# When a layer's state-space tables are built, and where its delta rule starts: one reordering inside a hybrid decoder layer

## The chip, the cores and the metric

The program runs on one core of a Trainium2 chip. The metric is the device time of one execution in microseconds. A core has five engines that take instructions in order, each from its own list: TensorE (PE, with its weight loads shown apart as PEld), VectorE (DVE), ScalarE (ACT), GpSimd (POOL) and SyncE (SP), which here issues the DMAs. They meet through semaphores: an instruction that waits holds up everything behind it on its own engine.

## The reference, cut to what matters

Two layers run over 512 positions of width 1024. In each layer a mixer splits one projection of the normalized input into four head groups, each 256 wide; an expert layer (PEER) with a large pair of tables follows, then a gated embedding. The PEER part fills most of the time and is not touched. The mixer is:

```
y_ret  = retention(rq, rk, rv, rg, ...)                 # group A
y_lru  = rglru(lg, lx, ...)                             # group B
y_s5   = s5(su, a_re, a_im, b.., c.., d, log_dt, glu..) # group C
y_gdn  = gated_deltanet(dqkv, db, da, dg, ...)          # group D
mixed = concatenate([rmsnorm(y, branch_norm[l, j]) for j, y in enumerate(groups)])
h = h + mixed @ w_out[l]
```

Group C (S5) is a diagonal complex recurrence. Its coefficients do not depend on the data, only on the layer's parameters: powers of exp(a dt), the input matrix B and the output matrix C multiplied by them. From these the kernel builds tables. Group D (the gated DeltaNet) needs the convolved q, k, v and two gate logits per head (db, da); it inverts a triangular matrix per chunk of 64 positions and then carries a state from chunk to chunk.

## The kernel before

All float32 products are made of three products of split halves (hi*hi, lo*hi, hi*lo), so a weight that is used has first been loaded into `wraw` and split by ACT (`whi`) and DVE (`wlo`). The work is written as Python generators: each `yield` ends a step, and `mix` takes steps from several generators in proportion to a weight (a weight of 2 has twice as many steps per round as one of 1). What `mix` and `take` write down is still reordered: the program is scheduled once, when it is built, so each engine's list is fixed before the run, and what an engine does at run time follows that list.

`mixer` (from L1723) makes one layer's mixer in two halves.

First half: `proj` multiplies z with 11 column blocks of `w_in`, 8 steps per block (`pj`, PSUM tiles `ps_j`). Each block hands its result to a consumer: blocks 1 to 3 to the convolution of q, k, v of D (`d_cons_qkv`), the fourth (column 2560) to the gates of D (`d_cons_g`), the next four to A, then B and, last, C. Beside it runs the first part of D (`gen_D` up to `d_prepared`, PSUM tiles `ps_d`) and of A.

Second half: C (`gen_C`, then `finish_T`), the rest of A, B, an embedding product (`gen_embed`) and the rest of D (tiles dX, dE, dAT, oD, PSUM `ps_d`). Then `residual` multiplies the four finished groups (`zm`) with `w_out` (PSUM `ps_r`) and adds to `h`; its banks are those of `ps_j`, so it begins when the work on those is done. Its first six row blocks (`early=6`) are those of A, B and C, which need nothing of D. The query projection of PEER (`ps_q`) follows.

The tables of C are made by `gen_Cprep` (the argument `prep`, L1094): some 165 DVE instructions with a few of the other engines, on tiles s5raw, sb, s5p, sp, sq. It saves them to a DRAM buffer `Td`; `c_load` (L1077, L1082) loads them back as `s5t`. Layer 0 has its `prep` inside the mixer's first half; layer 1's tables are made elsewhere, and its mixer has no `prep`. `take(pj, 2 + 24)` stands ahead of it: that is 26 of the projection's 90 steps, three blocks and the start.

gen_C uses the tables thus: products of the inputs by `s5t` (L356) with copies and transposes (L1269, L1273, L1276), complex rotations and two scans per half (DVE L341, L344, L347, L1287, tiles sx, sZ, zm), output products, transposes (L1308), a gate product (`gluw`), and a norm whose result `xb` is turned (L1047) into `zm`.

Of the kernel before, what the change touches and what calls it, by code (L numbers as in the profile page):

```python
# [25 lines left out]
D = 1024  # L26
# [165 lines left out]
def drain(*gens):  # L192

    live = [[g, w] for g, w in gens]
    while live:
        for e in list(live):
            for _ in range(e[1]):
                try:
                    next(e[0])
                except StopIteration:  # L200
                    live.remove(e)
                    break
# [39 lines left out]
class Ker:  # L242
# [201 lines left out]
    def proj(self, z, wap, blocks, pool, bank, wmax=256, lo_eng=None, per=2, early=0):  # L444
# [15 lines left out]
        def spl(x):  # L460
            if x // 2 >= NB:
                return
            n = blocks[x // 2][1]
            hi = pool.tile([P, 4, wmax], F32R, name="whi", tag="whi", bufs=3)
            lo = pool.tile([P, 4, wmax], F32R, name="wlo", tag="wlo", bufs=3)
            self.split(hi[:, :, :n], lo[:, :, :n], raws.pop(x)[:, :, :n], lo_eng if x % 2 == 0 else None)
            sp[x] = (hi, lo)
            load(x + self.WR)
# [41 lines left out]
        for i, (c0, n, kind, cons) in enumerate(blocks):  # L510
            if begun and i < 2:
                continue
            nj = n // P if kind == "C" else NTB
            for j in range(nj):
                ps = bank()
                for kd in range(KD):
# [3 lines left out]
                    f, e = kd == 0, kd == KD - 1  # L520
                    if kind == "C":
                        cs = slice(j * P, (j + 1) * P)
# [6 lines left out]
                    if e:  # L529
                        cons(j, ps)  # L530
                        if j == 0:
                            spl(2 * i + 2)
                    if (kd + 1) % (per if kind == "C" else 2 * per) == 0:
                        yield
# [858 lines left out]
    def gen_select(self, pool, rpool, bank_s, qT, subT, tb, res):  # L1393
# [58 lines left out]
        def tree(x, out, eng):  # L1452
            n = 16
            while n > 2:
                n //= 2
                eng.tensor_tensor(x[:, 0:n], x[:, 0 : 2 * n : 2], x[:, 1 : 2 * n : 2], op=ALU.add)
            eng.tensor_tensor(out, x[:, 0], x[:, 1], op=ALU.add)

        M = t2("tM", [16, P], BF16)
        W = t2("tW", [16, P], BF16)  # L1460
        W2 = t2("tW2", [16, P], BF16)
# [4 lines left out]
        yield  # L1466
        self.mul(v4(W), v4(M), perh(dl))
        tree(W, fl(sel[:, 0]), V)
        yield
        self.sub(fl(bv), fl(pf), st)  # L1470
        self.tt(M, over(bv), self.t_row, ALU.is_equal)
        self.mul(v4(W), v4(M), perh(sb[:, 1]))
        tree(W, fl(sel[:, 1]), V)
        yield
# [50 lines left out]
    def peer(self, l, z, sides, prep=None):  # L1525
# [3 lines left out]
        with ExitStack() as c0:  # L1529
# [6 lines left out]
            def cons(b0):  # L1536
                def f(j, ps):
                    self.mul(qT[:, b0 + j, :], ps, z.rb)
                return f

            pj = self.proj(z, self.ap["wq"][l], [(256 * i, 256, "C", cons(2 * i)) for i in range(4)], wp, lambda: qbank())
            self.take(pj, 2)
# [175 lines left out]

    PD, PC, BD = 0, 0, 4
    R2, RC2, LO = 0.7, 0.4, 0  # L1720
    R0, R1, RC, RA = 2, 2, 0.6, 0.4

    def mixer(self, l, z, Td, gain, opened, sides, Pd, prep=None):  # L1723
        sa, sb = sides
        self.l, self.z, self.a_ready, self.c_half, self.d_half = l, z, False, False, False
        win = self.ap["w_in"][l]
        with ExitStack() as c0:
            cm_ = c0.enter_context(ExitStack())
            mx = self.pool(cm_, "mx", sb)
            self.a_alloc(mx)  # L1730
            self.b_alloc(mx)
            self.c_alloc(mx)
            oC = self.xb.rearrange("p a b -> p (a b)").rearrange("p (t c) -> p t c", t=NTB)
            cd_, cj_ = c0.enter_context(ExitStack()), c0.enter_context(ExitStack())
            bd = banks(self.pool(cd_, "ppd", space=PSUM, side="right"), "d", self.BD)
            bj = banks(self.pool(cj_, "ppj", space=PSUM, side="left"), "j", 8 - self.BD)
            cD = cm_.enter_context(ExitStack())
            with ExitStack() as c1:
                dcp = self.pool(c1, "dcp", sa)
                self.d_alloc(mx, dcp)  # L1740
                wp = self.pool(c1, "wp", sa)
                self.cvpool = wp
                blocks = [(1792, 256, "C", self.d_cons_qkv(0)), (2048, 256, "C", self.d_cons_qkv(2)), (2304, 256, "C", self.d_cons_qkv(4)),
                          (2560, 264, "T", self.d_cons_g), (0, 256, "T", self.a_cons("q")), (256, 256, "T", self.a_cons("k")),
                          (512, 256, "T", self.a_cons("v")), (768, 256, "T", self.a_cons("g")),
                          (1280, 256, "C", self.b_cons_x), (1024, 256, "C", self.b_cons_g), (1536, 256, "C", self.c_cons)]
                pj = self.proj(z, win, blocks, wp, bj, wmax=264, lo_eng=self.G if prep is not None and self.LO else None)
                if prep is not None:
                    with ExitStack() as c2:
                        np_ = self.pool(c2, "np", sa)  # L1750
                        self.take(pj, 1)
                        first = lambda part: self.z_first(z, self.gain("mixg", l), bd, np_, part)
                        first(0)
                        self.load_mix(mx, l)
                        first(1)
                else:
                    self.load_mix(mx, l)
                self.take(pj, 2 + 24)
                with ExitStack() as c2:
                    self.rope_tables(mx, self.pool(c2, "pr", sb))  # L1760
                if prep is not None:
                    with ExitStack() as c2:
                        self.mix([(prep(self.pool(c2, "pk", sb), bd), 1), (pj, self.R0)])
                self.take(pj, 8)
                dp = self.pool(cD, "dp", sb)
                self.d_prepared = False
                D = self.gen_D(dp, dcp, bd)

                def d1():
                    while not self.d_prepared:  # L1770
                        self.take(D, 1)
                        yield

                def a1():
                    while not self.a_ready:
                        yield
                    yield from self.gen_A(mx, dcp, bj, self.aq)

                D1 = d1()
                self.mix([(pj, 1), (a1(), self.R2), (D1, self.R1, self.PD)])  # L1780
                drain((D1, 1))
            z.ctx.close()
            self.zm = Mixed(self.pool(c0, "zm", sa))
            self.oD = self.pool(c0, "od", sa).tile([P, NTB, 256], F32, name="oD")
            with ExitStack() as c1:
                cp = self.pool(c1, "cp", sa)
                self.c_load(cp, Td)
                oA, yB = self.aq, self.lg

                def c_():  # L1790
                    yield from self.gen_C(l, cp, bj, oC)
                    yield from self.finish_T(cp, bj, oC, 4, "C")

                def a_():
                    yield from self.norm_A(cp, oA)
                    yield from self.finish_T(cp, bj, oA, 0, "A")

                def b_():
                    yield from self.gen_B(l, cp, bj, yB)
                    yield from self.finish_B(cp, bj, yB)  # L1800

                def upto(g, flag):
                    while not getattr(self, flag):
                        self.take(g, 1)
                        yield

                C = c_()
                W = self.gen_embed(l, self.pool(c1, "em", sa), bj, Pd)
                self.mix([(upto(C, "c_half"), self.RC), (a_(), self.RA), (b_(), self.RA), (W, self.RA), (upto(D, "d_half"), 1)])
                drain((upto(D, "d_half"), 1))  # L1810
                self.mix([(C, self.RC2), (D, 1, self.PD)])
            wp = self.pool(c0, "rw", sa)
            pj = self.residual(self.zm, self.ap["w_out"][l], wp)
            self.take(pj, 2)
            cj_.close()
            with ExitStack() as c1:
                self.rbank = banks(self.pool(c1, "rp", space=PSUM, side="left"), "r", 8 - self.BD)
                self.take(pj, 8)
                drain((D, 1))
                cm_.close()  # L1820
                cd_.close()
                znew = opened()
                self.blockwise(pj, znew, gain, banks(self.pool(c1, "rt", space=PSUM, side="right"), "t", 2), wp, 0)
# [202 lines left out]
```

## Time and profile before

| | us |
|---|---|
| median of 3 runs | 3987.49 (3984.82 to 3992.34) |
| the profiled execution | 3988.84 |
| its span in the profile | 3987.0 |
| first projection of layer 0 to its q projection | 10.2 to 396.8 |
| first projection of layer 1 to its q projection | 1998.5 to 2360.1 |

The span is what the profile's time axis covers; 1.8 us of the time lie outside it. Rows below give start and length in us within it, and the tiles by the names of the program (output<-input). A row of one line and form may stand for several instructions in a row (x4). A bracket at the end tells how long the engine was idle before the row and what ended that.

### The profile page before, as it was taken

Reading aid. Unit: us, or ns where it says so; the run is one execution under the profiler, and the core shown is the slowest. Engines: PE = TensorE matmul, PEld = TensorE weight load, DVE = VectorE, ACT = ScalarE, POOL = GpSimd, SP = SyncE. Lnnn points to the kernel's source line nnn. Section 1 sums busy time; section 2 is a strip of 40 time slices with the busy share of each in tenths; the row PEclk is TensorE's granted clock in tenths of the full one; section 3 lists DMA queues with packets and bytes.
Section 4 is the critical chain, followed back from the end, with each engine's and each line's share of the span. In section 5 each row is a group of like instructions: output and inputs, shape, how many; then the busy total and the mean of one; then the engine's idle time right before and its main releaser. Section 6 shows DMA issues by size and latency. Waiting matters only on the chain.

```text
span 3987.0 us, 54319 instructions
## 1 busy us (share of the span) xinstructions
PE 3891.8 (98%) x20648; PEld 3231.3 (81%) x20648; DVE 2899.9 (73%) x5889; ACT 1533.8 (38%) x2245; POOL 552.0 (14%) x470
## 2 busy tenths in 40 slices
PE   7999999999999999999999999999999999999998
PEld 6878888878888888888898787777788888888887
DVE  9785899968888666555575769998588865555555
ACT  4454255652233232222443443566422222222223
POOL 4321000010001222222031210000100012222220
PEclk9999999999999999999999999999999999999999
DMA  4223255675653443333231133556756534333422
GB/s 146 71 78 106 77 198 177 241 269 184 202 170 121 145 129 130 122 111 121 82 102 59 58 122 103 191 209 232 247 184 201 166 102 136 110 121 108 134 83 90
DMA packets 317190, 562.33 MB, mean 141 GB/s; under 512 B 18176, under 2 KB 206720, under 8 KB 311552
## 3 DMA queue, kind: packets, MB, share of 16 engines
q1 hardware_dynamic: 316928, 558.86, 42.0%
q8 instruction: 162, 2.65, 0.3%
q14 instruction: 100, 0.82, 0.1%
HBM read 443.96 MB, written 114.83 MB: 140 GB/s over the span
## 4 chain that ended last, share of the span: by engine, by line
PE 87%; DVE 9%; DMA 2%; issue 1%; ACT 1%; POOL 0%; SPq 0%; DVEq 0%; POOLq 0%; ACTq 0%
PE ps_v L356 35%; PE ps_u L356 32%; PE ps_j L356 5%; PE ps_g L356 5%; PE ps_d L356 3%; PE ps_r L356 2%; PE ps_q L356 2%; DVE ulo L360 1%; DVE to L338 1%; PE ps_s L356 1%; DMA s5t<-Td 1%; DVE wlo L360 0%; DVE dc L350 0%; DMA wraw<-in_ple_wg_dram 0%; PE ps_t L373 0%
## 5 line engine op out<-in xcount | busy, mean ns | idle before, releaser
L1685 DVE TENSOR_TENSOR h<-h,ps_v 128x512 f32<-128x512 f32 x1024 | 678.0, 682 | 633.1 <-PE ps_v L356 631.9
L356 PE MATMUL ps_v<-vhi,whi 128*128 128x512 f32 x2048 | 800.6, 391 | 18.8 <-ACT whi L359 18.8
L356 PE MATMUL ps_u<-zhi,ulo 128*128 128x512 f32 x2048 | 812.9, 397 | 0.6 <-DVE ulo L360 0.6
L356 PE MATMUL ps_u<-zhi,uhi 128*128 128x512 f32 x2048 | 809.9, 395 | 0.4 <-ACT aout L353 0.4
L356 PE MATMUL ps_u<-zlo,uhi 128*128 128x512 f32 x2048 | 808.2, 395 | 0.0
L356 PE MATMUL ps_v<-vlo,whi 128*128 128x512 f32 x2048 | 800.3, 391 | 0.0
L356 PE MATMUL ps_v<-vhi,wlo 128*128 128x512 f32 x2048 | 796.4, 389 | 0.0
L360 POOL TENSOR_TENSOR ulo<-uraw,uhi 128x1024 fp32r<-128x1024 f32 x136 | 329.4, 2423 | 2191.1 <-ACT uhi L359 1614.3
L359 ACT CAST uhi<-uraw 128x1024 fp32r<-128x1024 f32 x256 | 269.7, 1054 | 854.5 <-PE ps_u L356 571.2
L359 ACT CAST whi<-dact 128x512 fp32r<-128x512 f32 x256 | 158.5, 620 | 818.4 <-issue 376.1
L356 PEld LDWEIGHTS ps_v<-vhi,whi 128*128 128x128 f32 x2048 | 385.5, 188 | 102.0 <-ACT whi L359 19.6
L356 PEld LDWEIGHTS ps_u<-zhi,ulo 128*128 128x128 f32 x2048 | 384.8, 188 | 84.2 <-DVE ulo L360 1.4
L356 PEld LDWEIGHTS ps_u<-zlo,uhi 128*128 128x128 f32 x2048 | 384.9, 188 | 83.5
L356 PEld LDWEIGHTS ps_u<-zhi,uhi 128*128 128x128 f32 x2048 | 384.9, 188 | 83.0 <-ACT aout L353 1.2
L356 PEld LDWEIGHTS ps_v<-vlo,whi 128*128 128x128 f32 x2048 | 385.9, 188 | 81.6
L356 PEld LDWEIGHTS ps_v<-vhi,wlo 128*128 128x128 f32 x2048 | 384.9, 188 | 81.2
L341 DVE TENSOR_TENSOR dact<-dact,dg 128x512 f32<-128x512 f32 x256 | 320.0, 1254 | 29.5 <-ACT dact L353 17.0
L360 DVE TENSOR_TENSOR vlo<-vraw,vhi 128x1024 fp32r<-128x1024 f32 x256 | 309.1, 1226 | 26.1 <-ACT vhi L359 26.1
L353 ACT ACTIVATE tstg<-ps_g 128x512 f32<-128x512 f32 x256 | 264.2, 1156 | 128.2 <-PE ps_g L356 126.1
L359 ACT CAST vhi<-vraw 128x1024 fp32r<-128x1024 f32 x256 | 261.6, 1048 | 21.8 <-PE ps_v L356 20.4
L360 DVE TENSOR_TENSOR wlo<-dact,whi 128x512 fp32r<-128x512 f32 x256 | 180.2, 706 | 37.1 <-ACT whi L359 24.1
L338 DVE TENSOR_TENSOR to<-t_iota,tii 128x1024 f16<-128x1024 bf16 x256 | 172.8, 685 | 2.0 <-ACT tii L353 1.7
(470 smaller groups left out, 5382.4 us busy)
## 6 DMA issues: line engine op xcount, KB each, us to landing
uraw<-in_uT_dram SPq DMA_DIRECT2D x256, 512.0 KB, 3.4
vraw<-in_v_dram SPq DMA_DIRECT2D x256, 512.0 KB, 3.9
Gd<-tstg SPq DMA_DIRECT2D x32, 2048.0 KB, 7.2
dg<-Gd SPq DMA_DIRECT2D x64, 1024.0 KB, 6.0
Ad<-aout SPq DMA_DIRECT2D x120, 256.0 KB, 2.2
dact<-Ad SPq DMA_DIRECT2D x120, 256.0 KB, 3.4
wraw<-in_w_in_dram SPq DMA_DIRECT2D x40, 512.0 KB, 3.6
wraw<-in_w_out_dram SPq DMA_DIRECT2D x16, 512.0 KB, 3.8
```

Of the source, the lines that this page charges most:

```text
L338: (eng or self.V).tensor_tensor(out, a, b, op=op)
L341: (eng or self.V).tensor_tensor(out, a, b, op=ALU.mult)
L353: self.A.activation(out, x, f, **k)
L356: self.PE.matmul(out, l, r, start=start, stop=stop)
L359: self.A.copy(hi, x)
L360: (lo_eng or self.V).tensor_tensor(lo, x, hi.bitcast(F32), op=ALU.subtract)
L1685: self.reached = V.tensor_tensor(self.h[:, tb, ds], self.h[:, tb, ds], ps, op=ALU.add).ins
```

## The change

In layer 0 the call that mixes `prep` with the projection goes away; so `take(pj, 8)` follows `take(pj, 2 + 24)` directly and D begins after 34 steps, right behind the block of its gates, where before at least 34 more steps lay between. `prep` now runs in the second half in a mix with A, B, the embedding and the first part of D's rest (`d_half`), with a weight of 0.6 in place of 2. Behind it stand, in a pool of their own, the loading of the tables and C. In layer 1, where `prep` is None, the same lines give nearly the same order as before.

```diff
-    R0, R1, RC, RA = 2, 2, 0.6, 0.4
+    R0, R1, RC, RA = 0.6, 2, 0.6, 0.4
...
-                if prep is not None:
-                    with ExitStack() as c2:
-                        self.mix([(prep(self.pool(c2, "pk", sb), bd), 1), (pj, self.R0)])
                 self.take(pj, 8)
...
-                self.c_load(cp, Td)
...
-                C = c_()
-                W = self.gen_embed(l, self.pool(c1, "em", sa), bj, Pd)
-                self.mix([(upto(C, "c_half"), self.RC), (a_(), self.RA), (b_(), self.RA), (W, self.RA), (upto(D, "d_half"), 1)])
-                drain((upto(D, "d_half"), 1))
+                Dh = (upto(D, "d_half"), 1)
+                gs = [(a_(), self.RA), (b_(), self.RA), (self.gen_embed(l, self.pool(c1, "em", sa), bj, Pd), self.RA)]
+                if prep is not None:
+                    with ExitStack() as c2:
+                        self.mix([(prep(self.pool(c2, "pk", sa), bj), self.R0)] + gs + [Dh])
+                    gs = []
+                cc = self.pool(c1, "cc", sa)
+                self.c_load(cc, Td)
+                C = c_(cc)
+                self.mix([(upto(C, "c_half"), self.RC)] + gs + [Dh])
+                drain(Dh)
                 self.mix([(C, self.RC2), (D, 1, self.PD)])
```

PE, DVE, POOL and SP issue the same instructions in both kernels; only the order differs.

TensorE's list in layer 0 before, in the stretch where the gate product of C and its turned result stand. Between the matmuls of C (`ps_j<-gluw`, `ps_j<-ca,xb`) lie those of D (`ps_d`), and those of the residual (`ps_r`) begin among D's.

```order
L356 MATMUL ps_j<-gluw,sx_2357 128x512 x5
L718 MATMUL ps_d<-ca,dX 128x128 x2
L356 MATMUL ps_d<-dX,dE 128x128 x2
...
L1047 MATMUL ps_j<-ca,xb 128x128 x4
L718 MATMUL ps_d<-ca,dX 128x128 x2
L1047 MATMUL ps_j<-ca,xb 128x128 x4
L356 MATMUL ps_d<-dX,dE 128x128 x2
L356 MATMUL ps_d<-dS,dwT 64x128
L356 MATMUL ps_d<-dAT,dX 128x128 x8
L356 MATMUL ps_d<-dS,dwT 64x128
L356 MATMUL ps_r<-whi,zm_2567 128x256 x4
L718 MATMUL ps_d<-ca,dX 128x128 x2
```

The same list in the change, from D's last rows to the residual's first. The lines left out repeat the first pair of C three times and its middle once.

```order
L356 MATMUL ps_d<-dvn,daT 64x64 x2
L820 MATMUL ps_d<-ca,oD 128x128 x4
L356 MATMUL ps_j<-s5t_2872,sx_2900 128x256 x2
L1273 MATMUL ps_j<-ca,sx_2899 128x128 x4
...
L356 MATMUL ps_j<-s5t_2875,su 128x128
L356 MATMUL ps_j<-s5t_2873,sZ 128x4x32 x8
L1308 MATMUL ps_j<-ca,sx_2900 128x128 x4
L356 MATMUL ps_j<-gluw,sx_2899 128x512 x8
L1047 MATMUL ps_j<-ca,xb 128x128 x8
L356 MATMUL ps_r<-whi,zm_2334 128x256 x4
L356 MATMUL ps_r<-wlo,zm_2334 128x256
```

All of C has moved behind D's last matmul (oD is D's result), and all 384 matmuls of the residual behind C; no matmul of D lies among either.

VectorE's list in layer 0 of the change, at the end of the table building (the last two rows that write s5p) and the beginning of C (sx, sZ, zm); `zm_2189<-ps_d` is D's finished result.

```order
L350 SCALAR_TENSOR_TENSOR zm_2189<-ps_d,gv,zm_2188 128x128 x2
L347 TENSOR_TENSOR s5p_2595<-sb_2198,sb_2199 128x8x64
L341 TENSOR_TENSOR sb_2198<-sp_2600,s5p_2595 128x512
L341 TENSOR_TENSOR sb_2199<-sq_2601,s5p_2595 128x512
L360 TENSOR_TENSOR wlo<-wraw,whi 128x1024
L344 TENSOR_TENSOR s5p_2595<-sb_2198,sb_2199 128x8x64
L360 TENSOR_TENSOR wlo<-wraw,whi 128x1024 x2
L1251 COPY sx_2900<-su 32x256 x4
L341 TENSOR_TENSOR sx_2899<-s5t_2877,zm_2898 128x512
L341 TENSOR_TENSOR sZ<-s5t_2877,zm_2897 128x512
```

The table building, which before ended in the first half, now ends behind D's last rows here; between it and C stand two splits and a copy.

SyncE's list in layer 0 of the change, around the last save of a table (`Td_65<-s5p`) and the loads of the tables.

```order
L457 DMA wraw<-in_wq_dram 128x4x256 x3
L1110 DMA Td_65<-s5p_2595 128x2048
L457 DMA wraw<-in_wq_dram 128x4x256 x2
L1077 DMA s5t_2873<-Td_65 128x2560
L1077 DMA s5t_2875<-Td_65 128x1024
L1077 DMA s5t_2877<-Td_65 128x2048
L1077 DMA s5t_2879<-Td_65 128x8
L1082 DMA s5t_2872<-Td_65 32x4x512 x4
L1236 DMA gluw<-in_glu_w_dram 128x2x512
```

Before, the saves stood among the weight loads of the projection, and seven other issues lay between the last of them and the first load of `s5t`; now two loads of weights lie between.

## Rows read from the trace of the kernel before

**Rows 1.** The page, busy time of each engine over the span.

```profile
PE 3891.8 (98%) x20648; PEld 3231.3 (81%) x20648; DVE 2899.9 (73%) x5889; ACT 1533.8 (38%) x2245; POOL 552.0 (14%) x470
```

**Rows 2.** Busy time by stretch, the mixers of both layers (header names the columns).

```profile
core 0: us, PE busy (x) PEld busy (x) DVE busy (x) ACT busy (x) POOL busy (x), PEclk, DMA share, GB/s
10.00:190.00 180.00, 164.86 (x1039) 143.03 (x1040) 151.36 (x371) 73.50 (x125) 68.31 (x78) 0.95 0.29 96
190.00:397.00 207.00, 193.45 (x1345) 166.46 (x1344) 144.54 (x319) 105.24 (x249) 40.58 (x54) 0.96 0.30 95
...
1997.00:2183.00 186.00, 183.98 (x1261) 166.16 (x1260) 118.67 (x256) 72.19 (x135) 45.08 (x59) 0.99 0.21 65
2183.00:2300.00 117.00, 102.06 (x629) 80.80 (x627) 92.35 (x206) 63.73 (x141) 31.72 (x30) 0.93 0.24 77
2300.00:2325.00 25.00, 23.62 (x174) 20.48 (x175) 14.25 (x37) 8.68 (x22) 3.86 (x6) 1.00 0.27 86
2325.00:2360.00 35.00, 35.00 (x297) 34.90 (x296) 21.61 (x36) 20.73 (x51) 0.52 (x4) 1.00 0.67 225
1997.00:2360.00 363.00, 344.66 (x2357) 302.34 (x2356) 246.88 (x534) 165.32 (x347) 81.17 (x99) 0.97 0.27 86
```

**Rows 3.** Timeline of VectorE, first and last rows of the table building.

```profile
22.84 1.39 DVE L341 TENSOR_TENSOR sb<-s5raw 128x136 f32<-128x136 f32 x1
...
114.88 0.69 DVE L344 TENSOR_TENSOR s5p<-sb,sb 128x512 f32<-128x512 f32 x1
```

**Rows 4.** Busy time by stretch, shorter ones, same columns as rows 2.

```profile
50.00:75.00 25.00, 20.42 (x134) 18.39 (x136) 24.83 (x50) 5.39 (x8) 10.36 (x12) 0.93 0.34 124
...
195.00:200.00 5.00, 2.31 (x15) 1.79 (x16) 4.95 (x15) 4.89 (x9) 1.11 (x2) 1.00 0.85 305
200.00:205.00 5.00, 4.58 (x28) 4.29 (x29) 4.48 (x14) 3.46 (x8) 0.00 (x0) 0.66 1.00 381
```

**Rows 5.** Timeline of TensorE: the rest of D in both layers; layer 0's q projection.

```profile
239.01 0.60 PE L356 MATMUL ps_d<-dX,cb 128*128 128x256 f32 x2
...
366.46 0.44 PE L820 MATMUL ps_d<-ca,oD 128*128 128x128 f32 x2 [1.20 <-ACT oD L353]
...
396.77 0.48 PE L356 MATMUL ps_q<-zhi,whi 128*128 128x512 f32 x1
...
2176.76 0.59 PE L356 MATMUL ps_d<-dX,cb 128*128 128x256 f32 x2
...
2328.13 0.38 PE L820 MATMUL ps_d<-ca,oD 128*128 128x128 f32 x2
```

**Rows 6.** DMA issues, 100 to 125 us: KB each, us to landing.

```profile
Td<-s5p SPq DMA_DIRECT2D x1, 1024.0 KB, 5.4
```

**Rows 7.** Timelines of SyncE and TensorE, the tables' first load and first use.

```profile
195.10 2.14 SPq L1077 DMA_DIRECT2D s5t<-Td  x4
...
211.39 0.89 PE L356 MATMUL ps_j<-s5t,sx 128*128 128x256 f32 x3 [0.90 <-DMA s5t<-Td]
```

**Rows 8.** Timelines of ScalarE and VectorE in C, first copy to last rotation.

```profile
212.53 0.59 ACT L1269 COPY sx<-ps_j 128x512 f32<-128x512 f32 x1 [2.17 <-PE ps_j L356]
...
227.92 0.69 DVE L341 TENSOR_TENSOR sx<-s5t,zm 128x512 f32<-128x512 f32 x1 [1.54 <-PE ps_j L1273]
...
262.28 0.65 DVE L344 TENSOR_TENSOR sZ<-sZ,sx 128x508 f32<-128x508 f32 x1
```

**Rows 9.** Timeline of TensorE, from C's output products to the residual's first.

```profile
283.77 0.28 PE L356 MATMUL ps_j<-s5t,sZ 128*128 128x128 f32 x1
283.89 1.50 PE L356 MATMUL ps_d<-dAT,dX 128*128 128x128 f32 x12
...
306.58 0.74 PE L356 MATMUL ps_r<-whi,zm 128*128 128x256 f32 x4
```

**Rows 10.** TensorE's busy time, 205 to 306 us, on s5t, then on gluw.

```profile
205.00:306.00 101.00, 14.14 (x64) 0.95 0.19 55
...
205.00:306.00 101.00, 7.20 (x16) 0.95 0.19 55
```

More of the change, by code (lines that the diff above doesn't have):

```diff
@@ L1786, in mixer, with c_ @@
                 cp = self.pool(c1, "cp", sa)
-                self.c_load(cp, Td)
                 oA, yB = self.aq, self.lg
-                def c_():
-                    yield from self.gen_C(l, cp, bj, oC)
+                def c_(pool):
+                    yield from self.gen_C(l, pool, bj, oC)
                     yield from self.finish_T(cp, bj, oC, 4, "C")
```

## The prediction

> **What bounds the kernel now.** I read the page's engine line first: TensorE is busy for 3891.8 of 3987.0 us [rows 1], so a mixer can only win or lose where TensorE stands still, and whatever the change does is added to the end. The change touches the mixer of layer 0, so I next read busy time by stretch there, beside the mixer of layer 1, which is the best witness: it has no table building in it, and its first half already has the structure that the change gives to layer 0. Layer 0 takes 180 + 207 = 387 us from its first projection to its q projection, layer 1 takes 363 [rows 2]. VectorE is busy for 151.4 + 144.5 = 295.9 us in the one and 246.9 in the other; the difference, 49.0 us, is what the table building costs VectorE, with 68.3 + 40.6 - 81.2 = 27.7 us of GpSimd [rows 2]. On VectorE it runs from 22.8 to 115.6 us [rows 3], and VectorE is full there, with 24.8 of 25 us from 50 to 75, while TensorE has 20.4 [rows 4]. So today the table building makes the first half of layer 0 bound by VectorE for a while, and the price of it in total is 387 - 363 = 24 us. That is the most that hiding it better could give.
>
> The second half of the mixers is not idle either. From 190 to 397 us VectorE has 144.5 of 207 us, TensorE 193.5 [rows 2]. TensorE's work there is a mixture: the chain of D, the chain of C, and the residual, of which those row blocks that need only A, B and C fill the gaps that D's chain leaves. The rest of D takes from 239.0 to 366.9 us, 128 us, in layer 0, and from 2176.8 to 2328.5, 152 us, in layer 1 [rows 5]; it is a chain of small products and copies, and without filler TensorE would wait in it.
>
> **The change, part by part.** I build the time of the q projection in layer 0 anew; it stands at 396.8 us now [rows 5].
>
> *First half.* It loses the table building, and D's first half starts earlier. Layer 1 shows such a half: 186 us with TensorE busy for 184.0, so it is full [rows 2]. No earlier start of D can gain there, since the products themselves fill it. Layer 0 begins at 10 us at a lower granted clock (0.95 over its first half against 0.99) [rows 2]; scaled by the clocks the 186 us would be 194. Part of that lower clock comes from the building itself, so I take 190, and 200 us for the end of the first half, between 196 and 204. That is 10 us later than the 190 of today: more of D's first half now lies ahead of that point, and this is not lost, since D's second half starts with it done.
>
> *Second half up to D's end.* The work on VectorE: layer 1 has 92.4 + 14.3 = 106.6 us between 2183 and 2325 [rows 2]. C's rotations, scans and the rest of C are out of that (I add its rows to 29 us: the rotations and scans, 23 us of them, lie between the last two of [rows 8]), and so are the splits of `w_out` (5 us), which the new order puts behind. 73 us are left, and the table building adds 49: 122 us. Where VectorE was full it was so to 99% [rows 4], but the building ends in chains with D, A and B beside it, so I add 9 us for gaps: 131 us. The lower bound is 117 us (nothing but VectorE's work, with a little of it hidden behind the end), the upper 144, by D's 152 us in layer 1 less the 6 us by which it began ahead of the half's end [rows 5]. It ends at 331 us. GpSimd's 28 us are hidden by VectorE's.
>
> *C alone.* This is the term that decides. The order puts all of C behind the last of D on TensorE, and behind the building on VectorE. The residual's banks follow C, so nothing of it can fill either. C then runs as one chain:
> - the last table is saved to DRAM, and the load must wait for it: 5.4 us to landing [rows 6];
> - the tables come back: 16.3 us from the first load's issue (195.10) to the first product with them (211.39) [rows 7]. Today these lie beside the last projections; in the change nothing else is ready;
> - four rounds of a product, a copy and transposes, 1.73 us each (from 211.39 to the copy's end at 213.12) [rows 7, 8]: 6.9 us;
> - rotations and scans: 22 DVE rows from 227.9 to 262.9 us, whose lengths add to 23.1 us [rows 8]. GpSimd shares them out, D's work lies between them. In the change VectorE has little else, so I take 23 and not the 35 us that passed;
> - output products, gate product, norm and turning, from 283.8 to the residual's first product at 306.6: 22.8 us, of which about 3.9 are D's products between (the row of 1.50 us and some smaller ones) [rows 9]: 19 us.
>
> The sum is 5.4 + 16.3 + 6.9 + 23 + 19 = 70.6, say 70 us, to 401 us. The bounds are 52 us (the load has been issued early enough to be half done, and a third of the rotations goes to GpSimd) and 80 (chains at a lower clock and with waits). TensorE has 14.1 us of products with the tables in it, 7.2 of the gate product [rows 10] and 4 to 5 of transposes: some 26 us.
>
> The clock adds to this. When TensorE is busy for 2.3 of 5 us (195 to 200), the next 5 us are granted 0.66 of full speed [rows 4], which is a mixture of the levels of 1.2 and 2.4 GHz. I put the loss into the upper bound, since most of C's chain is not TensorE's. The Trainium skill, "TensorE: Matmul & The Clock Gate", section "HAM oscillation — how this bites in real kernels", says that a TensorE that idles between bursts is put back to half rate and pays for warming anew each time; the rows of this trace agree with that, and by the rule, as an estimate from its two rates, C's 26 us of products could take up to twice that, 26 us more than my sum.
>
> The two DMAs of the table's way over DRAM can't overlap, in the sum: the Trainium skill, "DMA: Bandwidth & Descriptors", section "Two DMAs through the same engine are not ordered", says that only the completion of the first orders a second one that reads what it wrote. No run here shows what happens without; the sum with an overlap would be 5 us less.
>
> *The residual.* 384 products and 32 transposes stand behind C, and they are nobody's cover any more. Saturated, 297 such rows take 35.0 us in layer 1 [rows 2], 0.118 us each: 416 take 49 us. With 4 us for the first block's additions and the last block's norm I take 53 us (49 to 58). Today a third to a half of it lies in D's gaps: only 30 us pass from D's last rows (366.5) to the q projection (396.8) [rows 5].
>
> *The sum:* 200 + 131 + 70 + 53 = 454 us against 396.8: 57 us later. PEER behind it has the same work in almost the same order, and so has layer 1, so I give them nothing. The saved table loads of ScalarE (three fewer activation tables, of 51) are on an engine with 179 of 387 us [rows 2], hidden. Against the profiled execution of 3988.8 us, which is 1.3 us over the median, 57 us are 4045.8, and **4045 us** against the median.
>
> **The rivals.**
>
> *It gets faster.* The second half has 62.5 us in which VectorE is idle (207 - 144.5) [rows 2], and 49 us of building fit there. If C were hidden as it is in layer 1, the mixer would come to layer 1's 363 us and the cold start's 4 to 8, thus to 379-386 us: 11 to 18 us earlier, 3971 to 3978 us. The first half speaks for that, where VectorE at 24.8 of 25 us holds TensorE back [rows 4]. The order speaks against it: the idle time of VectorE would have to lie ahead of D's end, and C is behind D. It decides for this if D's chain is itself held by C's and the residual's products on TensorE so that it would end some 60 us earlier without them. Its VectorE work of 122 us after 200 forbids nearly all of that.
>
> *C is short.* The building ends early beside D (117 us), the tables are back before D's end, and C alone takes 52 us: 196 + 117 + 52 + 53 = 418, 21 us later, some 4010 us. For it speaks that the bounds are from rows with other work beside them; against it that the building's last row stands behind D's last rows on VectorE.
>
> *All is worse.* D and the building are a chain of 144 us, and C takes 80 at a lower clock, the residual 58: 204 + 144 + 80 + 58 = 486, 89 us later, some 4077 us. For it speaks layer 1, where D took 152 us [rows 5] at a granted clock of 0.93 [rows 2].
>
> *No change,* where the gains of the first half just pay for C: it needs C to be hidden but for some 15 us, and nothing in the order allows that.
>
> **How the numbers follow.** The main case, with its own range of 4028 to 4062, has 0.62; C short 0.14; all worse 0.15; faster 0.05; no change 0.04. The likeliest gives 4045 us. The range leaves out the two cases without a loss (0.09) and a part of the outer ones: 4010 to 4078. By 0.2% I mean 8 us, about what a measurement of this kernel can tell from no change. Faster 0.05, same 0.04, slower 0.91.
>
> **What would show it.** In the profile of the changed kernel the last projection should stand near 200 us; VectorE should be full from there to about 330, with the last row of the building near D's last; then a stretch of about 70 us in which TensorE is busy for a third, begun by a wait of some 20 us for the tables from DRAM, then a full stretch of about 50 us of residual, and the q projection near 454. I am wrong if C's first product comes well ahead of 330, if TensorE is busy for most of C's stretch, or if the first half ends well below 190.

## The result, and the profile after

The change takes 4046.85 us (median of 4 runs, 4045.57 to 4047.99) against 3988.67 us before: a ratio of 1.0146, 95% interval 1.0134 to 1.0158, so 58.2 us slower. 4045 us had been predicted. The profiled execution took 4047.99 us, with a span of 4046.2 us.

The page's engine line of the change, against [rows 1]: TensorE has 13 us more busy time (its mean granted clock was 0.979 against 0.988), and the span is 59 us longer. TensorE does the same 20648 products and stands still for longer between them.

```profile
PE 3904.9 (97%) x20648; PEld 3239.9 (80%) x20648; DVE 2893.4 (72%) x5889; ACT 1533.0 (38%) x2242; POOL 548.4 (14%) x470
```

Busy time by stretch of layer 0's mixer in the change, cut where its chain changes hands: end of the projection, end of the building, first product of C, end of its four rounds, end of the rotations, first product of the residual, first q projection. The columns are those of [rows 2].

```profile
10.00:202.00 192.00, 187.04 (x1253) 167.48 (x1254) 131.19 (x278) 78.10 (x144) 57.48 (x67) 0.99 0.24 74
202.00:318.40 116.40, 90.57 (x601) 68.95 (x599) 107.20 (x339) 55.70 (x134) 30.65 (x37) 0.91 0.17 62
318.40:341.70 23.30, 0.01 (x1) 0.04 (x1) 4.21 (x7) 6.14 (x9) 3.78 (x5) 0.50 0.99 304
341.70:351.70 10.00, 7.91 (x28) 5.20 (x28) 0.69 (x1) 3.70 (x9) 1.27 (x1) 0.69 0.01 3
351.70:370.40 18.70, 3.09 (x12) 2.63 (x12) 18.64 (x19) 2.52 (x4) 11.96 (x7) 0.67 0.00 0
370.40:399.80 29.40, 19.86 (x72) 12.99 (x72) 10.97 (x22) 12.88 (x25) 1.03 (x1) 0.73 0.24 81
399.80:453.50 53.70, 52.82 (x416) 52.10 (x417) 20.52 (x32) 18.22 (x44) 1.64 (x10) 0.94 0.35 119
```

Read it downwards. First TensorE is full, then VectorE nearly is (107.2 of 116.4), then TensorE stands still and VectorE nearly does (4.2 us busy) for 23.3 us in which the DMA works at a share of 0.99 (304 GB/s), then VectorE is full (18.6 of 18.7, with 12.0 of GpSimd beside it) while TensorE has 3.1, and only the last stretch fills TensorE again, with 416 matmuls.

The handovers in the timelines of the change (TensorE, GpSimd, VectorE, SyncE), against [rows 3, 5 to 9]:

```profile
201.33 0.40 PE L356 MATMUL ps_j<-zhi,wlo 128*128 128x512 f32 x1
201.55 2.24 POOL L1112 MEMSET s5p<- 128x2560 f32 x1 [2.23 <-PE ps_j L356]
201.76 0.69 DVE L341 TENSOR_TENSOR su<-ps_j,zrb 128x512 f32<-128x512 f32 x1 [6.80 <-PE ps_j L356]
205.66 1.04 DVE L341 TENSOR_TENSOR sb<-s5raw 128x136 f32<-128x136 f32 x2
312.46 0.69 PE L820 MATMUL ps_d<-ca,oD 128*128 128x128 f32 x2 [4.07 <-DVE sq L344]
317.29 1.12 DVE L344 TENSOR_TENSOR s5p<-sb,sb 128x512 f32<-128x512 f32 x1
318.44 0.34 SPq L1110 DMA_DIRECT2D Td<-s5p  x1
320.01 3.78 SPq L457 DMA_DIRECT2D wraw<-in_wq_dram  x2
324.15 1.84 SPq L1077 DMA_DIRECT2D s5t<-Td  x4
341.69 2.04 PE L356 MATMUL ps_j<-s5t,sx 128*128 128x256 f32 x4 [28.54 <-DMA s5t<-Td]
399.82 1.28 PE L356 MATMUL ps_r<-whi,zm 128*128 128x256 f32 x4 [3.58 <-ACT whi L359]
453.50 0.48 PE L356 MATMUL ps_q<-zhi,whi 128*128 128x512 f32 x1
```

The building's first real step waits for the projection's last product: GpSimd's clearing of a table starts 0.2 us after it is issued. The reload, from the building's end to C's first product, is seen in the chain of waits (start, length, what):

```profile
317.40 3.66 DMA wraw<-in_wq_dram
321.09 1.05 ACT whi L359
322.17 1.23 DVE wlo L360
323.42 4.47 DMA wraw<-in_wq_dram
327.90 13.66 DMA s5t<-Td
341.69 2.06 PE ps_j L356 x4
```

Two loads of the q projection's weights (`wraw`) lie in it ahead of the tables. From 315 to 342 us the DMA moved 7.1 MB: 3.9 are the tables, 1.6 three such weight loads, 1.0 the save and 0.5 `gluw`.

Where the 56.7 us of the mixer (453.5 against 396.8) come from: C's first product is 130.3 us later than before (341.7 against 211.4 [rows 7]). C itself, from that product to the residual's first, takes 58.1 us in place of 95.2, with none of D's products in it: 37.1 us given back. The residual takes 53.7 in place of 90.2 us (306.6 to 396.8 [rows 5, 9]), also without D: 36.5 us given back. 130.3 - 37.1 - 36.5 = 56.7. Behind the q projection the change loses another 2.5 us.

### The profile page after: what moved, and what is told of

Read it like the earlier page. It is cut to its first block, busy times and chain, and to the rows that moved or that the text cites. A ratio compares the mean times of both kernels' runs of the same rounds, so it can differ in the third digit from the quotient of the medians.

```text
span 4046.2 us, 54326 instructions
## 1 busy us (share of the span) xinstructions
PE 3904.9 (97%) x20648; PEld 3239.9 (80%) x20648; DVE 2893.4 (72%) x5889; ACT 1533.0 (38%) x2242; POOL 548.4 (14%) x470
## 4 chain that ended last, share of the span: by engine, by line
PE 89%; DVE 7%; DMA 2%; ACT 1%; issue 1%; SPq 0%; POOL 0%; DVEq 0%; POOLq 0%; ACTq 0%
PE ps_v L356 34%; PE ps_u L356 33%; PE ps_j L356 7%; PE ps_g L356 5%; PE ps_d L356 3%; PE ps_q L356 2%; PE ps_r L356 2%; PE ps_s L356 1%; DVE ulo L360 0%; DMA wraw<-in_ple_wg_dram 0%; PE ps_t L373 0%; PE ps_d L718 0%; DVE wlo L360 0%; DVE dc L350 0%; DVE to L338 0%
## 5 line engine op out<-in xcount | busy, mean ns | idle before, releaser
L360 DVE TENSOR_TENSOR wlo<-wraw,whi 128x1024 fp32r<-128x1024 f32 (+1 forms) x92 | 118.6, 1291 | 77.0 <-ACT whi L359 76.7
```

The lines of the kernel that those rows point to most:

```text
L360: (lo_eng or self.V).tensor_tensor(lo, x, hi.bitcast(F32), op=ALU.subtract)
```

## The experiments

Each ran with runs of the kernel before on the same chip; the ratios are to those.

**The building ahead of everything else.** The edit writes the building first and C beside D again; what the scheduled order made of it is read below.

```diff
-                        self.mix([(prep(self.pool(c2, "pk", sa), bj), self.R0)] + gs + [Dh])
-                    gs = []
+                        drain((prep(self.pool(c2, "pk", sa), bj), 1))
```

> The change, but with the tables built ahead of everything else in the second half, and A, B, the embedding and D's rest mixed with C behind it, as before the change: C's products stand among D's again. Theory (C and the residual lie bare behind D): the building costs about 50 to 60 us at the head of the second half, then D's 128 us cover most of C, so the q projection comes near 400 to 415 us and the time is 3995 to 4010 us. Rival (VectorE is the bound of the second half, wherever the building stands): the q projection stays near 450 us and the time at 4040 to 4050 us.

4046.01 us, 1.0145 (1.0128 to 1.0161): the change's own time, and the rival's. Busy time by stretch, cut at the building's end, C's first product, the residual's first, the q projection:

```profile
201.00:297.00 96.00, 75.15 (x467) 58.79 (x465) 86.60 (x302) 29.96 (x90) 22.86 (x32) 0.80 0.10 39
297.00:315.80 18.80, 0.00 (x0) 0.01 (x1) 2.73 (x4) 4.31 (x7) 3.56 (x6) 0.50 0.87 288
315.80:401.80 86.00, 53.72 (x251) 39.56 (x251) 56.87 (x81) 48.52 (x87) 22.36 (x13) 0.78 0.27 88
401.80:455.00 53.20, 51.90 (x415) 51.10 (x416) 20.16 (x31) 18.12 (x44) 2.10 (x15) 0.96 0.34 113
```

TensorE's work on D's tiles (`ps_d`) alone, in this run beside the building and beside C, then in the change beside the building:

```profile
201.00:297.00 96.00, 73.27 (x432) 0.80 0.10 39
315.80:401.80 86.00, 3.36 (x22) 0.78 0.27 88
202.00:318.40 116.40, 71.27 (x453) 0.91 0.17 62
```

The building ends 21 us earlier than in the change, so C begins 26 us earlier. But D stayed where it was: 432 of its products ran beside the building, and only the last 22 beside C. What moved to C is A, B and the embedding, and C's stretch grows from 58.1 to 86.0 us. So the run does not put C back among D, and the theory, that C is long because it lies bare of D, is not tested by it. The rival, that VectorE's total is the bound, gave the time rightly, yet VectorE is idle for a third of C's stretch (56.9 of 86.0 busy), so its reason isn't shown either. What the run does show: taking A, B and the embedding from the building's side gains 26 us there and costs 28 in C.

The reload is shorter here, 18.8 us. No weight load lies ahead of the tables, and the first load's issue (301.24) comes when the save, issued at 296.92, has landed 4.2 us later.

**D late again, the building left where the change has it.**

```diff
-                self.take(pj, 8)
+                self.take(pj, 8 if prep is None else 42)
```

> The change with D started late again: 42 steps of the projection in place of 8 are taken ahead of it, so D begins after 68 steps; the building stays in the second half. Theory (TensorE fills the first half whatever D does): within 8 us of the change, 4039 to 4055 us. Rival (the early D gains time that the second half gives back): 10 to 25 us slower than the change, 4057 to 4072 us.

4024.27 us, 1.0089 (1.0072 to 1.0106): 22.6 us faster than the change. Both expectations are missed, and on the other side: the early D costs. Its stretches, cut at the same handovers:

```profile
10.00:181.60 171.60, 163.09 (x1034) 142.39 (x1035) 112.76 (x213) 65.58 (x108) 54.88 (x66) 0.97 0.27 83
181.60:293.00 111.40, 96.55 (x683) 78.72 (x681) 108.22 (x341) 53.73 (x127) 20.00 (x24) 0.95 0.16 56
293.00:319.70 26.70, 22.92 (x118) 15.71 (x116) 14.96 (x45) 12.61 (x35) 9.10 (x15) 0.75 0.65 207
319.70:381.90 62.20, 33.41 (x137) 23.72 (x136) 39.05 (x64) 26.15 (x56) 16.58 (x12) 0.75 0.25 82
381.90:435.40 53.50, 52.83 (x417) 52.24 (x417) 20.56 (x32) 18.14 (x44) 1.69 (x12) 0.94 0.36 118
```

The projection ends at 181.6 us, 20 us before the change's, and the building, whose first clearing starts at 181.5 us, ends at 293.0, 25 us before. C begins at 319.7, 22 us before, and the q projection comes at 435.4, 18 us before. D's last product comes at 337.0 us in place of 312.7, and the time is shorter all the same. New theory: one chain sets the end, the projection's end, the building, the reload, C, the residual; D's products that are put ahead of the projection's end delay it.

D is not quite off that chain. The tables had landed by 314 us (the DMA is idle from there on), and C's first product came 6 us later, straight behind products of D on TensorE's list. And the gain can be told from TensorE's side as well: 22.9 us of D's products fill the reload, in which TensorE stands still in the change. The runs don't separate the two ways of telling it.

**No building, and no building with D late.** The first stores zeros in place of layer 0's tables; the second adds the edit of `take` (42) to it.

```diff
+    def stub(self, pool, Td):
+        t = pool.tile([P, 2560], F32, name="s5z")
+        self.G.memset(t, 0.0)
...
-            self.mixer(..., Pd, prep(0) if l == 0 else None)
+            self.mixer(..., Pd, (lambda pool, bank: self.stub(pool, Td[0])) if l == 0 else None)
```

> The kernel before, with layer 0's tables not computed: zeros are stored to DRAM in their place, so the output of S5 in layer 0 is left out. D begins after some 46 steps of the projection. Theory (the building costs layer 0 what separates the two mixers, 24 us, less a colder start): the q projection at 377 to 386 us, the time 3966 to 3978 us. Rival (the building was hidden before): within 8 us of before, 3980 to 3996 us.

3982.56 us, 0.9984 (0.9974 to 0.9993). Without the building the kernel before is 6 us faster (3 to 10), not 24: the rival's number, in the main. D starts earlier in this run than in the kernel before (after 46 steps in place of 68), so the 6 us hold that too.

> As the run without the building, but with D begun after some 80 steps of the projection. Theory (an early D gains nothing in itself, since TensorE fills the first half): within 8 us of that run, 3960 to 3984 us. Rival (the early D is worth something once the building is away): 10 to 25 us slower than that run.

3976.58 us, 0.9972 (0.9961 to 0.9982), 12 us (7 to 16) below the kernel before and 6 below the first run, as the theory had it. The intervals of the two overlap, so what an early D costs without a building (some 6 us) is not shown. For the change the two runs say that there were only some 6 to 12 us to be had from hiding the building better, however well it had gone.

Busy time of layer 0's mixer in the two runs, columns of [rows 2]:

```profile
10.00:388.70 378.70, 356.54 (x2349) 308.87 (x2349) 258.54 (x528) 175.73 (x358) 92.31 (x118) 0.95 0.30 96
10.00:383.30 373.30, 350.06 (x2349) 303.07 (x2349) 254.63 (x528) 170.39 (x354) 92.25 (x118) 0.98 0.31 98
```

VectorE has 37 to 41 us less here than in the kernel before (295.9 us [rows 2]). That is the building's price on VectorE, where the difference of the two layers had said 49.

**A shorter building.** The last table of layer 0 is zeroed in place of being computed by doublings.

```diff
+        if not l:
+            G.memset(p[3], 0.0)
...
-        for k in (2, 4, 8, 16, 32, 64):
+        for k in (2, 4, 8, 16, 32, 64) if l else ():
```

> The change, with the doublings of the last table left out in layer 0 (the table is zeroed instead, so S5's result there is not computed): 58 VectorE rows of 17.1 us busy that lie from 278 to 318 us, 40 us of the building's end. Theory (one chain in a row sets the end: projection's end, building, reload, C, residual; D is beside it): C begins some 30 us earlier until D's end at 313 us gets into it, so the time is 25 to 38 us shorter, 4009 to 4022 us. Rival (the second half is bound by VectorE's work): worth the busy time at most, 17 us, 4030 to 4040 us.

4011.09 us, 1.005 (1.0035 to 1.0065): 35.8 us faster than the change by the medians (32 by the profiled executions). VectorE has 72 instructions less (5817 against 5889), whose lengths in the change add to 18 us; so they were worth about twice that, as the chain theory said. Cut at the projection's end, C's first product, the residual's first:

```profile
200.70:308.40 107.70, 93.18 (x574) 71.71 (x572) 89.09 (x249) 52.66 (x123) 34.37 (x39) 0.86 0.31 108
308.40:367.50 59.10, 32.84 (x144) 23.17 (x143) 39.37 (x65) 27.39 (x59) 16.65 (x12) 0.76 0.27 88
367.50:420.90 53.40, 52.63 (x417) 52.04 (x417) 20.44 (x32) 18.03 (x44) 1.66 (x10) 0.94 0.34 116
298.00:308.40 10.40, 9.46 (x39) 6.32 (x39) 5.70 (x19) 3.00 (x9) 3.17 (x7) 0.53 0.00 1
```

The last save is issued at 279.2 us, 39 us earlier. C begins 33.3 us earlier (308.4 against 341.7), with D still running beside it until 331, and C and the residual behind take what they take in the change (59.1 and 53.4 against 58.1 and 53.7). The last row is the stretch just ahead of C: the DMA moves nothing any more, and TensorE is busy with D's products. So here C waits for its place behind D on TensorE's list and not for the tables, as the expectation allowed ("until D's end at 313 us gets into it").

**The building's weight at 2.**

```diff
-    R0, R1, RC, RA = 0.6, 2, 0.6, 0.4
+    R0, R1, RC, RA = 2, 2, 0.6, 0.4
```

> The change, with the building's weight in the mix of the second half at 2, as it was before, in place of 0.6. Theory (one chain in a row, and VectorE's list hardly moves, as the building still competes with D): 4040 to 4050 us. Rival (the weight of 0.6 made the building late): the building ends 30 us or more earlier and the time is 4010 to 4025 us.

4035.17 us, 1.0122 (1.0107 to 1.0138): 11.7 us faster, between the two expectations. The last step of the building starts at 313.7 us in place of 317.3 and the projection ends 3 us earlier; C begins at 335.1. So the weight is a small part of it. One of its four times (4043.14) lies 8 us above the others, and its interval touches the change's (1.0134 to 1.0158), so the size is uncertain. The q projection comes at 446.8, 6.7 us earlier; the other 5 us lie behind the mixer and were not looked into.

**D later still, the building in the second half.** 54 steps in place of 8.

> The change with 54 steps of the projection in place of 8 ahead of D, so D begins after 80 of 90 steps. Theory (the building starts with the projection's end, and D is beside that chain): the projection ends near 166 us, 16 us earlier than with 42 steps, but nearly all of D now competes with the building on VectorE, so the building takes 5 to 15 us longer; the time is 0 to 12 us shorter than with 42 steps, 4012 to 4025 us. Rival (with D so late its own chain ends last): 4026 to 4045 us.

4032.79 us, 1.0116 (1.0099 to 1.0133): no faster than with 42 steps, some 8 us slower by the medians, with intervals that overlap; in the profiled executions the q projection comes at 433.5 against 435.4. The time is the rival's, but D's last product comes at 325.8 us, well ahead of C's end, so D's own chain does not end last. Stretches, then the projection's last product and the building's first steps on GpSimd and VectorE:

```profile
10.00:150.00 140.00, 135.30 (x848) 120.42 (x848) 92.28 (x162) 57.28 (x90) 38.41 (x44) 1.00 0.31 91
150.00:296.60 146.60, 130.79 (x915) 106.44 (x915) 128.97 (x401) 61.87 (x153) 37.91 (x48) 0.93 0.14 52
296.60:320.00 23.40, 18.48 (x91) 13.04 (x90) 14.67 (x47) 12.53 (x32) 8.19 (x13) 0.66 0.72 237
149.74 0.40 PE L356 MATMUL ps_j<-zhi,wlo 128*128 128x512 f32 x1
169.47 2.23 POOL L1112 MEMSET s5p<- 128x2560 f32 x1
182.67 0.51 DVE L341 TENSOR_TENSOR sb<-s5raw 128x136 f32<-128x136 f32 x2
```

The projection ends another 32 us earlier, but the building does not start with it: its first clearing comes 20 us behind the projection's last product, and its first computing step on VectorE at 182.7 us, only 5 us earlier than with 42 steps (187.5). From that step to its end it takes 114 us in place of 106, within the 5 to 15 us more that the theory allowed. So what the theory had wrong is the start. In the kernel's text the building's memory is that of the whole first half, D's first part included; that this is what holds the start here fits, but was not tested. An earlier end of the projection is worth something only as long as it is what the building waits for.

**The load from another buffer.** The tables are loaded from a second buffer in DRAM, filled with zeros in the first half; this was to take away the wait for the save.

```diff
+                    if prep is not None:
+                        drain((self.stub(self.pool(c2, "pz", sb), self.Tz), 1))
...
-                self.c_load(cc, Td)
+                self.c_load(cc, Td if prep is None else self.Tz)
```

> The change, with the tables of layer 0 loaded from a second DRAM buffer that was filled with zeros in the first half, so that the load need not wait for the last save; the building still runs and saves, and the load still waits for the building's memory. S5's result in layer 0 is not computed rightly. Theory (one chain; the reload is bound by its bytes, 3.9 MB, and its place behind two weight loads): 1 to 6 us shorter than the change, 4041 to 4046 us. Rival (the tables' way over DRAM is the wait that sets C's begin): 15 to 23 us shorter, 4024 to 4032 us.

4050.14 us, 1.0153 (1.0136 to 1.017): no gain, and both expectations are missed. SyncE's rows, what the first load waited for (us in all, times, longest), and the save's us to landing:

```profile
321.34 0.34 SPq L1118 DMA_DIRECT2D Td<-s5p  x1
322.91 3.83 SPq L457 DMA_DIRECT2D wraw<-in_wq_dram  x2
327.35 1.86 SPq L1077 DMA_DIRECT2D s5t<-Tz  x4
SPq L1077 <- DMA Td<-s5p: 0.5, 1, 0.5
Td<-s5p SPq DMA_DIRECT2D x1, 1024.0 KB, 6.0
```

The edit did not take the wait away. The load still waits for the building's memory, and the save reads from that memory: it lands at 321.34 + 6.0 = 327.3 us, and the load is issued at 327.35. So the run itself settles nothing about the save, and the rival stands untested by it. The trace of the change says how much this wait alone can be worth there: the save lands at 324.1 us (318.44 + 5.7), the second weight load ahead has been issued by 323.8, and the tables' first load comes at 324.15. As an estimate from these, the load would have come 0.3 us earlier without this wait, far from the rival's 15 to 23. What the save and the two weight loads cost together was not tried.

**D's place in the kernel before.** Two runs there: D later (20 steps in place of 8 ahead of it), and D earlier (the weight R0 at 0.6, so that fewer steps are written beside the building).

> The kernel before, with 20 steps of the projection in place of 8 taken ahead of D, so D begins after some 80 of 90 steps in place of 68. Theory (products of D that run before the projection's end delay all that waits for that end): the projection ends some 5 to 10 us earlier and the time is 0 to 8 us shorter, 3980 to 3988 us. Rival (before, D's own chain ends last): D ends later and the time is 5 to 15 us longer, 3993 to 4003 us.

3995.59 us, 1.0016 (1.0007 to 1.0025): slower by 2.8 to 10 us, the rival. The projection ends at 166 us, 25 us earlier, but D's last product comes 4 us later: in the kernel before it is D that ends last.

> The kernel before, with the building's partner weight at 0.6 in place of 2: some 10 steps of the projection are written beside the building in place of 34, so D begins after about 44 steps in place of 68; the building stays in the first half. Theory (an earlier D delays the projection's end and what waits for it): 4 to 12 us longer, 3992 to 4000 us. Rival (an earlier D helps where the building is not behind it): 3 to 10 us shorter, 3978 to 3985 us.

3997.93 us, 1.0024 (1.0015 to 1.0033): slower, as the theory said. The projection ends at 212 us, 20 us later, C begins at 233.2 in place of 211.4, D's last product comes at 374.4 in place of 366.6, and the q projection at 404.2.

## Why the prediction came out right

The time came out within 2 us, and the terms of its sum against the trace of the change are:

| | predicted | its range | measured |
|---|---|---|---|
| end of the first half | 200 | 196 to 204 | 201.7 |
| to the end of the building | 131 | 117 to 144 | 116.7 |
| C alone, with the reload | 70 | 52 to 80 | 81.4 |
| residual | 53 | 49 to 58 | 53.7 |
| q projection | 454 | | 453.5 |

Two of the four are off by 11 to 14 us, just outside their own ranges, in opposite directions. That the sum is right to half a microsecond is luck. That building, reload, C and residual stand one behind the other, as the sum has them, is not.

**The first half: right in size, wrong in meaning.** The prediction said that the 10 us by which the projection ends later are "not lost, since D's second half starts with it done". They are lost: with D late the projection ends 20 us earlier and the kernel is 22.6 us faster. This is a step that failed. It looked at D, which ends last in the kernel before but does not set the end in the change; the building starts with the projection's last product here, and so does the chain that ends last.

**The second half up to the building's end.** It took the prediction's lower bound (117), not the 131 us. I had read it as VectorE's work, 122 us of it; VectorE's busy time there was 107.2 us. The building's 49 us, taken from the difference of the two layers, were too many: the runs without it say 37 to 41. Nor is it VectorE's total alone that counts: the building is a chain of small steps that shares VectorE with D, and taking some 18 us of them from its end gave 36 us back.

**C alone.** The reload took 23.3 us against 5.4 + 16.3; the rounds 10.0 against 6.9; the rotations 18.7 against 23; the rest 29.4 against 19. What lies from the output products on is the part most mis-sized; TensorE waits there 4.6 us for the norm on ScalarE and 3.6 us for the split of the first weights of `w_out` (the row at 399.82 above). TensorE's 30.9 us of busy time from 341.7 to 399.8 are 5 us above the 26 that were counted; the granted clock there was 0.67 to 0.73, between its two levels. The Trainium skill, "TensorE: Matmul & The Clock Gate", section "HAM oscillation — how this bites in real kernels", says that a TensorE with idle gaps is put back to half rate; the trace agrees, with the clock at 0.50 in the reload, where TensorE did nothing for 23 us, and those values behind it. Of the 26 us more that the rule allowed as an upper estimate, 5 came.

**The order.** That all of C and all of the residual would stand bare behind D held, and so did the sum by stretches. What the runs show to be on the path is the late start of C, 130 us, of which 74 come back because C and the residual are no longer shared with D: a building that ends 39 us earlier brings C forward by 33 us and the end by 32 to 36. Whether C would be cheaper among D's products with the building left in the second half is not shown, as no run put it there. The prediction's "nothing of it can fill either" was said of the residual; the run with D late again shows that D's products, started later, do fill the reload.

**The rivals.** Faster, by 11 to 18 us, had next to no room: with no building at all the gain is 3 to 10 us, with D late as well 7 to 16. The estimate of 24 us for the building's whole price, from the difference of the two mixers, was two to four times too high: without a building layer 0's mixer still takes 373 to 379 us against layer 1's 362, for reasons that were not looked into. Two sums of the prediction don't come out as written, and neither decides anything: 363 us and 4 to 8 more end at 377 to 381, not 379 to 386, and 152 less 6 is 146, not 144.

By parts, in this order: the building's move with its new weight costs 35.6 us (4024.27 - 3988.67, with D started where it was), the early D another 22.6. In the kernel before, a D that starts after 44 steps costs 9 us. Where the 2.5 us behind the mixer come from stays open; the order in layer 1 differs by small exchanges, and the runs above vary there by several us.

None of the runs that compute the whole result beats the kernel before.

## What to carry to other kernels

Before work is moved, ask what starts when the engine that it leaves or joins reaches a barrier: a pool whose memory comes free, or the end of a projection. Work that is put ahead of a barrier and isn't awaited behind it delays everything that is, and clearing it away helps only until something else holds the barrier. And price "what the work costs today" by a run without it: here the difference between two similar stages said 24 us where the runs said 6 to 12. And look in the trace whether an edit did what it was meant to do: two of the edits here left in place what they should have moved, and their times alone would have been read wrongly.

## What the hardware showed that I had not expected

The reload in the change keeps the DMA full: from 318.4 to 341.7 us its engines were busy to 0.99 at 304 GB/s while none of the five engines was busy for more than 6.1 us of it. Some three of its 7.1 MB are not the tables'; in the run with the building first, which has no weight loads ahead of them, it took 18.8 us at a share of 0.87.

And 72 VectorE instructions, whose lengths add to 18 us, were worth 39 us at the end of the building and 36 of the time. In the change they stretch from 271.1 to 318.4 us, 47 us, with D beside them until 313; in the run with the building first, with less beside them, they take 28 us (268.7 to 296.9).
